# The last head's prompt output row moved into the samples' row of score sums, and the samples' new tokens summed in their output row

## The chip, the cores and the metric

The kernel runs on one core of one Trainium2 chip. The metric is the device time of one execution in microseconds (us). Five engines run side by side, each through its own queue in order: PE (TensorE, matmuls, with weight loads shown apart as PEld), DVE (VectorE), ACT (ScalarE), POOL (GpSimd) and SP (SyncE, which here only issues DMAs). They wait for one another by semaphores.

## The reference, cut to what matters

One layer of a decoder is computed for a prompt of 256 tokens and for 8 samples of 4 new tokens each (32 rows), with the same weights. One projection gives the inputs of a gated short convolution (mixer A), the queries, keys and values of a dilated windowed attention (mixer B), and two gates. Mixer B has 3 groups of 4 heads of 128 features; a head's output is merged over the three groups by their softmax denominators, which is one softmax over the keys of all three groups. A prompt token attends to prompt tokens. A sample's token attends to the sample's cached keys and to its own new tokens:

```python
kg = jnp.concatenate([kv_prev[g][:, :, 0].astype(x.dtype), kg], axis=1)
vg = jnp.concatenate([kv_prev[g][:, :, 1].astype(x.dtype), vg], axis=1)
o, l = _dilated_band_sample(q[:, :, g], kg, vg, slopes[g], dil)
wg = jax.nn.softmax(jnp.stack(lses), axis=0)
yb = jnp.einsum('gnth,gnthd->nthd', wg, jnp.stack(outs)).reshape(n, t, ATT_OUT).astype(x.dtype)
```

The rest of the layer takes `yb` into a product with `w_branch_b`, then come `w_out`, a layer norm, a gated feed-forward part and a second norm. All inputs are float32.

## The kernel before, in words

**The products.** Nearly all of the time goes into products of weights with the 288 token columns (256 of the prompt, 32 of the samples). Each weight block is 128 outputs by up to 2048 inputs. To keep float32 accuracy each operand is split into a high and a low part, and `mms` (L237) makes three matmuls for each 128 by 128 piece: high with high (L243), high with low (L244), low with high (L245). `product` (L225) takes the next prepared block, prepares another with `prepare` (L185), lets one step of the samples' attention be issued (`next(steps)`), issues the matmuls, and then calls `prompt_step` (L216).

**The weights' way.** `prepare` issues the load of a block by SP into one of three `wst` buffers. In two halves of 1024 columns ACT casts the high part and DVE subtracts to get the low part (`split`, L248, shown at L249), into four `whi` and four `wlo` buffers. A cast can be made as soon as PE has used the half four before it. When casts or subtractions come late, PE stands at L243 or L245.

**The order of the work.** A planner orders each engine's instructions before the run, by the order in which the program gives them and by expected times; the order is then fixed. `behind` and `in_a_row` fix the order of two instructions on one engine by hand. Work beside the products is issued in portions: each product's `prompt_step` issues up to `N_MOVES` (7) items from two lists, `soon` first, then `some_time` (`some_moves`, L209), and takes the prompt's attention one stage further.

**The prompt's attention** (`prompt_attention`, L466) runs head by head while the keys and values of the next head are projected. For a head it issues a row of score matmuls (L478), and in the same row on PE the output matmuls of the head before (`output_row`, L430, L439). Softmax follows. Values and weights are then turned for the output: DVE transposes 32 by 32 blocks (`squares`, L448), and the blocks are moved to their places (`moved`, L460): of sixteen blocks four on the diagonal by POOL, twelve by ACT (L458), which go into `soon`. The output row's result is copied from PSUM by ACT (L444), turned by DVE, moved by twelve DVE copies (L456, in `some_time`) and split into `ybh` and `ybl`. The last of the four heads has no successor, so its output row stands alone on PE (L524), and its moves are not portioned out: twice `some_moves(len(soon))` (L514, L519) issues all that is waiting. It runs while the first products of mixer A's convolution stage go on.

**The samples' attention** (`sample_steps`, L575) is a list of steps, one to a product, from the last query products on until its output row at 666 us in the trace. Cached keys are multiplied by the queries on ACT and POOL (L562, L564) and folded by DVE (L570). `key_sums` (L604) sums over the feature quarters on PE (L599) and scores the new keys (L612), both in one row on PE. `scores` makes the softmax, `weights_by_key` turns the weights. `new_values` turns the new tokens' values into `vn`, `new_output` (L652) multiplies them by their weights in a row of its own (L655), ACT copies the result (`o_sb`), `output_by_feature` turns it by sixteen DVE transposes (L410) into `oT`. Then the cached values are treated as the keys were, and `output` (L660) sums their quarters on PE (L599), adds `oT` on DVE (L666) and splits the samples' columns of `ybh` and `ybl`.

**Memory.** `dd_all` holds 4608 columns of 128 partitions: two buffers `kv` of a head's keys and values (columns 0 to 3456, the second, used by the last head, from 1728 on) and `sw[0]` behind them. `sw[1]` is a tile of its own. Both `sw` hold the samples' sums and weights in turn. After a head's projection ACT issues the DMAs that send its keys and values out (L765, L766).

Of the kernel before, what the change touches and what calls it, by code (L numbers as in the profile page):

```python
# [12 lines left out]
AF = mybir.ActivationFunctionType  # L13
ALU = mybir.AluOpType
# [3 lines left out]
P = 128  # L18
# [63 lines left out]
LATER = 3  # L82

N_MOVES = 7

# [13 lines left out]
def layer_kernel(ctx: ExitStack, tc: tile.TileContext, ins, outs):  # L101
# [103 lines left out]


    soon, some_time = [], []

    def some_moves(n):  # L209
        for _ in range(n):  # L210
            for todo in (soon, some_time):
                if todo:
                    todo.pop(0)()
                    break

    def prompt_step():  # L216
        some_moves(N_MOVES)
        if prompt[0]:
            prompt[1] -= 1
            if prompt[1] <= 0:  # L220
                prompt[1] = next(prompt[0], None)
                if prompt[1] is None:
                    prompt[0] = None
# [186 lines left out]
                behind(dve.transpose(out[b : b + 32, :, a : a + 32], src[a : a + 32, :, b : b + 32]), w_split[1])  # L410
            yield

    def to_features(j):

        squares(o_squares, o_two)
        for c in range(NC):
            to = oT.rearrange("p (a h i c) -> p a c h i", a=2, h=2, c=NC // 2)[:, c % 2, c // 2]
            for d in range(0, P, 32):
                move(some_time, (c * 32, d), to[d : d + 32], o_squares[c * 32 : (c + 1) * 32, :, d : d + 32], True)
        some_time.append(lambda: split(h2(ybh[:, j])[:, :, :P], h2(ybl[:, j])[:, :, :P], h2(oT)))  # L420
# [8 lines left out]

    def output_row():  # L430

        j, v, sums = o_next.pop()
        po = sb(ps, [P, SEQ], "acc")
        row = []
        for h in range(2):
            for b in range(2 + h):
                for c in range(NC):
                    at = slice(c * NW, (c + 1) * NW)
                    row.append(pe.matmul(  # L439
                        po[at, h * P : (h + 1) * P], sT[:, 2 * h + b, at], v[:, b if b <= h else 2 + c],  # L440
                        start=b == 0, stop=b == 1 + h,
                    ))
        for h in range(2):
            act.activation(o_two[:, h], po[:, h * P : (h + 1) * P], AF.Copy, scale=sums[h])  # L444
        to_features(j)
        return row

    def squares(out, src):  # L448
# [11 lines left out]
    def moved(out, src):  # L460

        for a in range(0, P, 32):
            for b in range(0, P, 32):
                move(soon, (a, b), out[b : b + 32, :, a : a + 32], src[a : a + 32, :, b : b + 32])

    def prompt_attention(j, q, kT, vT, k_class):  # L466

        s3 = [att((2 + h) * P) for h in range(2)]
        row = [last_mm[0]]

        for h in range(2):
            near = (1 + h) * P
            for g in range(NG):
                for c in range(NC):
                    at = slice(c * NW, (c + 1) * NW)
                    keys, k = (far_keys(h, g), k_class[g - 1][:, c, : (1 + h) * NW]) if g else (
                        slice(0, near), kT[:, 0, :near])
                    row.append(pe.matmul(  # L478
                        s3[h][at, keys], q[:, g, h * P + c * NW : h * P + (c + 1) * NW], k, start=True, stop=True
                    ))  # L480
        if o_next:
            some_moves(len(soon))
            row += output_row()
        in_a_row(row)
        s_flat = s_all.rearrange("p b k -> p (b k)")
        s = [s_flat[:, : 2 * P], s_flat[:, 2 * P :]]
        pool.memset(s[0][:, P:].rearrange("p (g k) -> p g k", g=NG - 1)[:, :, NW:], -BIG)
        for h in range(2):
            near = (1 + h) * P
            for g in range(NG):  # L490
                at = far_keys(h, g) if g else slice(0, near)
                dve.scalar_tensor_tensor(
                    s[h][:, at], m_far[:, h, g - 1, : (1 + h) * NW] if g else m_near[h], -SLOPE[g][j] / SCALE,
                    s3[h][:, at],
                    ALU.mult, ALU.add,
                )
        sums = []
        for h in range(2):
            st = sb(wk, [P, 4], "st", bufs=4)
            dve.reduce_max(st[:, 0:1], s[h], AX.X)  # L500
            dve.tensor_scalar_mul(st[:, 1:2], st[:, 0:1], -SCALE)
            act.activation(s[h], s[h], AF.Exp, bias=st[:, 1:2], scale=SCALE, accum_out=st[:, 2:3])
            dve.reciprocal(st[:, 3:4], st[:, 2:3])
            sums.append(st[:, 3:4])
        v = v_two[j % 2]
        squares(v_squares[:, :2], vT[:, 0, :SEQ].rearrange("p (b k) -> p b k", b=2))
        for g in range(1, NG):
            squares(
                v_squares[:, 2:, (g - 1) * NI : g * NI].rearrange("p c (h i) -> p c h i", i=32),
                vT[:, g, :SEQ].rearrange("p (h i c) -> p c h i", h=2, c=NC),  # L510
            )
        moved(v, v_squares)
        if j == NH - 1:
            some_moves(len(soon))  # L514
        yield 1
        squares(s_squares, s_all)
        moved(sT, s_squares)
        if j == NH - 1:
            some_moves(len(soon))  # L519
        yield 2  # L520

        o_next.append((j, v, sums))
        if j == NH - 1:
            in_a_row([last_mm[0]] + output_row())  # L524


    dd_all = sb(big, [P, KD * T], "dd")
    kv = dd_all[:, : 2 * 2 * NG * T].rearrange("p (b c g t) -> p b c g t", b=2, c=2, g=NG)
    sw = [dd_all[:, 2 * 2 * NG * T :], sb(wk, [P, (NB + 1) * NH * NS], "sw", bufs=1)]

    n_half = NH * NT * P // 2
    halves = [dd_all[:, h * n_half : (h + 1) * n_half] for h in range(2)]
# [42 lines left out]
    def sample_steps():  # L575
# [3 lines left out]
        s_key = sw[0][:, : (NG + 1) * P].rearrange("p (g r) -> p g r", r=P)  # L579
        sT, sTn = s_key[:, :NG], s_key[: NG * NS, NG]  # L580

        vn = dd_all[: NG * NS, 2 * n_half : 2 * n_half + NH * P].rearrange("p (j d) -> p j d", j=NH)
        o_sb = sw[0][:, NG * P + P + NH * P : NG * P + 2 * P + NH * P]
        oT = sw[1][:, NB * P :]

        n = NH * NQ * NS
        sums_k, sums_v = (
# [16 lines left out]
        def key_sums():  # L604
            pk = att(NG * P)
            row = []
            for g in range(NG):
                row += four_parts(pk[:, g * P : (g + 1) * P], sums_k[g], start=True, stop=True)

            ps_s.append(att(NG * NS))  # L610
            row += [
                pe.matmul(  # L612
                    ps_s[0][j * NS : (j + 1) * NS, k * NS : (k + 1) * NS], q_s[:, k, j, :],
                    k_s[:, k, j, :], start=True, stop=True,
                )
                for k in range(NG) for j in range(NH)
            ]
            in_a_row([last_mm[0]] + row)
            act.copy(by_key, pk)
# [26 lines left out]
        def new_values():  # L646
            yield from turned(vn, v_s.rearrange("p j g r -> p j (g r)"), NG * NS)

        def output_by_feature():
            yield from turned(oT.unsqueeze(1), o_sb.unsqueeze(1))  # L650

        def new_output():  # L652
            p = att(P)
            in_a_row([last_mm[0]] + [
                pe.matmul(p[j * NS : (j + 1) * NS], sTn[:, j * NS : (j + 1) * NS], vn[:, j, :], start=True, stop=True)  # L655
                for j in range(NH)
            ])
            act.copy(o_sb, p)

        def output():  # L660
            po = att(P)
            row = [last_mm[0]]
            for g in range(NG):
                row += four_parts(po, sums_v[g], start=g == 0, stop=g == NG - 1)
            in_a_row(row)
            dve.tensor_tensor(oT, oT, po, ALU.add)  # L666
            split(*(h3(t)[:, :, :, P:] for t in (ybh, ybl)), oT.rearrange("p (j a h) -> p j h a", j=NH, h=2))

        for i, o in enumerate(range(0, P, 32)):
            if i == 1:  # L670
# [36 lines left out]
        for which, order in (("ck", far + near), ("cv", near + far)):  # L707
            for i, (n, t) in enumerate(order):
                for h in range(2):
                    when = now + (2 * i + h) * PACE[0] // PACE[1]  # L710
                    if t == h == 0:
                        at(when - LATER, load, which, n)
                    at(when, multiply, u, h, which, n, t)
                    at(when + 1, fold, u, h)
                u += 1
            if which == "ck":
                for d, what in ((2, key_sums), (4, scores), (9, new_output)):
                    at(when + d, what)
                for d, blocks in (
                    ((-6, -5, -4), new_values), ((3, 3, 4, 4), scores_by_row), ((6, 6, 7, 7), weights_by_key),  # L720
                    ((10, 11, 12, 13), output_by_feature),
                ):
                    what = by_fours(blocks)
                    for n in d:
                        at(when + n, what)
                now = when + 9
# [597 lines left out]
```

## Time and profile before

Three runs took 1708.12 to 1709.82 us, with a median of 1709.02.

| What | us |
|---|---|
| profiled execution, its own time | 1709.05 |
| its span in the trace | 1707.3 |
| PE busy | 1699.9 |
| DVE busy | 1192.2 |
| ACT busy | 941.3 |
| POOL busy | 387.6 |

The granted TensorE clock is 0.999 of full speed. A matmul of 288 columns shows 0.29 us from start to modelled end, but the next starts 0.12 us after it: matmuls overlap in the pipeline, so the cost of a matmul is read from the distance of starts, and not from its duration. In a row of the timeline stand the start and the length of a stretch of like instructions, the engine and line, the operation, the tiles (output, arrow, inputs), the shapes and the count, and in square brackets the engine's idle time before it with what ended it. In the prompt's part (about 100 to 250 us) ACT is busy 18 to 19 us of 20 in several stretches; DVE has 19.86 of 20 at 260 to 280 us.

### The profile page before, as it was taken

The numbers are of one execution on the slowest core, as the hardware profiler recorded it, in microseconds if no ns is written. First come the engines' busy times: TensorE is split into PE (matmuls) and PEld (weight loads), VectorE is DVE, ScalarE is ACT, GpSimd is POOL, SyncE is SP. The second block draws the span as 40 slices with busy tenths as digits, with TensorE's granted clock in tenths as the row PEclk, the third lists the DMA queues.
The fourth block names the chain that finished last, engine by engine and source line by source line (L and its number), as shares of the span: only waits on it lengthen the run. The fifth ranks groups of instructions, "written<-read, shape, count | busy, mean of one in ns | idle before, by whom it ended". The sixth has DMA issues, their size and how long they took to land.

```text
span 1707.3 us, 34334 instructions
## 1 busy us (share of the span) xinstructions
PE 1699.9 (100%) x14148; PEld 1694.4 (99%) x14148; DVE 1192.2 (70%) x1575; ACT 941.3 (55%) x1665; POOL 387.6 (23%) x510
## 2 busy tenths in 40 slices
PE   9999999999999999999999999999999999999998
PEld 9999999999999999999999999999999999999998
DVE  5477889978887675455788887855686554555575
ACT  5578876645666564444546555543555443344454
POOL 1123333202222210001453332300111100011164
PEclk9999999999999999999999999999999999999999
DMA  8788877676778886677766666666666566666663
GB/s 297 287 298 316 335 304 265 235 280 249 272 292 335 326 310 249 222 261 253 274 236 226 228 247 230 229 233 222 228 231 257 222 229 238 249 223 231 223 242 135
DMA packets 59068, 436.16 MB, mean 255 GB/s; under 512 B 7648, under 2 KB 11232, under 8 KB 19168
## 3 DMA queue, kind: packets, MB, share of 16 engines
q1 hardware_dynamic: 57472, 429.85, 67.6%
q10 hardware_dynamic: 1440, 4.13, 0.7%
q8 instruction: 110, 1.80, 0.4%
q14 instruction: 46, 0.38, 0.1%
HBM read 427.50 MB, written 94.53 MB: 306 GB/s over the span
## 4 chain that ended last, share of the span: by engine, by line
PE 98%; ACT 1%; DVE 1%; DMA 0%; issue 0%; SPq 0%; DVEq 0%
PE acc L243 32%; PE acc L245 32%; PE acc L244 32%; PE acc L331 1%; DMA wst<-in_w_in 0%; ACT yal L458 0%; DVE wlo L249 0%; PE acc L439 0%; PE att L478 0%; ACT yah L458 0%; ACT whi L249 0%; DVE dd L570 0%; PE long L978 0%; DVE yah L990 0%; PE acc L985 0%
## 5 line engine op out<-in xcount | busy, mean ns | idle before, releaser
L249 DVE TENSOR_TENSOR wlo<-wst,whi 128x1024 fp32r<-128x1024 f32 (+1 forms) x578 | 738.1, 1280 | 405.2 <-ACT whi L249 402.1
L249 ACT CAST whi<-wst 128x1024 fp32r<-128x1024 f32 (+1 forms) x578 | 588.6, 1021 | 679.9 <-PE acc L244 611.0
L243 PE MATMUL acc<-xh,whi 128*128 128x288 f32 (+1 forms) x3216 | 921.1, 286 | 0.0
L245 PE MATMUL acc<-xh,wlo 128*128 128x288 f32 (+1 forms) x3216 | 920.5, 286 | 0.4 <-DVE wlo L249 0.4
L244 PE MATMUL acc<-xl,whi 128*128 128x288 f32 (+1 forms) x3216 | 920.3, 286 | 0.0
L243 PEld LDWEIGHTS acc<-xh,whi 128*128 128x128 f32 x3216 | 607.8, 189 | 1.3 <-issue 1.2
L245 PEld LDWEIGHTS acc<-xh,wlo 128*128 128x128 f32 x3216 | 607.8, 189 | 0.8 <-DVE wlo L249 0.8
L244 PEld LDWEIGHTS acc<-xl,whi 128*128 128x128 f32 x3216 | 607.8, 189 | 0.0
L245 PE MATMUL acc<-yah,wlo 128*128 128x288 f32 x1216 | 347.7, 286 | 0.0
L244 PE MATMUL acc<-yal,whi 128*128 128x288 f32 x1216 | 347.7, 286 | 0.0
L243 PE MATMUL acc<-yah,whi 128*128 128x288 f32 x1216 | 347.6, 286 | 0.0
L245 PEld LDWEIGHTS acc<-yah,wlo 128*128 128x128 f32 x1216 | 229.8, 189 | 0.0
L244 PEld LDWEIGHTS acc<-yal,whi 128*128 128x128 f32 x1216 | 229.8, 189 | 0.0
L243 PEld LDWEIGHTS acc<-yah,whi 128*128 128x128 f32 x1216 | 229.8, 189 | 0.0
L794 POOL COPY qk_s<-u 128x2 f32<-128x2 f32 x44 | 36.8, 836 | 535.5 <-ACT u L1083 412.7
L782 DVE SCALAR_TENSOR_TENSOR cy<-u,prm,cy 128x304 f32<-128x304 f32 x120 | 72.6, 605 | 5.6 <-ACT cy L780 2.4
L564 POOL TENSOR_TENSOR cache<-cache,dd 128x1024 f32<-128x1024 f32 x16 | 34.1, 2134 | 93.4 <-DMA cache<-in_cv 55.8
L249 ACT CAST yah<-ya 128x288 fp32r<-128x288 f32 x76 | 32.6, 429 | 27.5 <-DVE ya L805 11.1
L564 POOL TENSOR_TENSOR cache<-cache,qk_s 128x1024 f32<-128x1024 f32 x16 | 32.7, 2045 | 53.7 <-DMA cache<-in_ck 40.6
L853 POOL TENSOR_TENSOR ya<-ya,dd 128x288 f32<-128x288 f32 x16 | 13.7, 858 | 133.8 <-DVE ya L852 132.8
L775 POOL COPY u<-prm 128x16 f32<-128x16 f32 x60 | 42.2, 704 | 4.6 <-DMA prm<-in_prm 4.6
L562 ACT ACTIVATE cache<-cache,qk_s 128x128 f32<-128x128 f32 x128 | 40.8, 392 | 0.0
(224 smaller groups left out, 1190.8 us busy)
## 6 DMA issues: line engine op xcount, KB each, us to landing
wst<-in_w_in SPq DMA_DIRECT2D x112, 1024.0 KB, 5.0
wst<-in_w_up SPq DMA_DIRECT2D x88, 1024.0 KB, 4.9
wst<-in_w_down SPq DMA_DIRECT2D x32, 1024.0 KB, 4.9
cache<-in_ck SPq DMA_DIRECT2D x18, 1024.0 KB, 7.8
cache<-in_cv SPq DMA_DIRECT2D x18, 1024.0 KB, 8.5
wst<-in_w_a SPq DMA_DIRECT2D x16, 1024.0 KB, 4.9
wst<-in_w_out SPq DMA_DIRECT2D x16, 1024.0 KB, 4.9
wst<-in_w_down SPq DMA_DIRECT2D x16, 768.0 KB, 4.4
```

The source lines that it names most:

```text
L243: pe.matmul(out, hi[:, c, :], xh_k, start=k == 0, stop=False)
L244: pe.matmul(out, hi[:, c, :], xl_k, start=False, stop=False)
L245: last_mm[0] = pe.matmul(out, lo[:, c, :], xh_k, start=False, stop=k == nk - 1)
L249: return act.copy(hi, src), dve.tensor_tensor(lo, src, f32(hi), ALU.subtract)
L331: i = pe.matmul(o[b], first_w(term == 2, b, k), xk, start=k == 0 and term == 0, stop=k == KD - 1 and term == 2,)
L562: behind(act.activation(o[:, a, b], t[:, a, b], AF.Copy, scale=w[:, a, b : b + 1]), w_split[0])
L564: behind(pool.tensor_tensor(o, t, w.unsqueeze(3).broadcast_to([P, *n]), ALU.mult), w_split[1])
L775: pool.tensor_copy(tail[:, :, 0:2], prm[:, state : state + 2 * NB].rearrange("p (b r) -> p b r", b=NB))
L782: dve.scalar_tensor_tensor(y, u[:, i : i + YW], prm[:, w0 + i : w0 + i + 1], y, ALU.mult, ALU.add)
L794: pool.tensor_copy(dst[:, 0:2], u[:, SEQ : SEQ + 2])
L853: pool.tensor_tensor(m, m, ma[:, i], ALU.add)
```

## The change

Three things are done together.

- The last head's output row no longer stands alone. Its moves go through the lists as those of the other heads. `key_sums` first issues whatever is left in the lists, then puts the output row ahead of its own row on PE. For that the last head's turned weights and values get a place that lives on: `late_p` and `late_v` in `dd_all`, columns 2048 to 3456; and the output's intermediate tiles one in `sw[0]` and `sw[1]` (`late_homes`). From then on `prompt_step` issues three items a product (`N_LATE`). A new step, `prompt_features`, issues what is left of them six steps later.
- `new_output` and `output_by_feature` go, with `o_sb` and `oT`. In `output`, after the quarters of the first group, sixteen matmuls add the new tokens' part directly, by feature, into the same PSUM tile (four heads by four blocks of 32 features). The addition on DVE goes; the split reads PSUM.
- `vn` moves from `dd_all` to the place of the samples' queries and keys (`qk_s`), and is made later: at steps 10 to 12 after the last key fold in place of 6 to 4 ahead of it.

```diff
 N_MOVES = 7
+N_LATE = 3
...
     def prompt_step():
-        some_moves(N_MOVES)
+        some_moves(N_LATE if all_heads[0] else N_MOVES)
...
-        j, v, sums = o_next.pop()
+        j, v, p, sums = o_next.pop()
+        homes = late_homes if j == NH - 1 else (o_two, o_squares, oT)
...
-                        po[at, h * P : (h + 1) * P], sT[:, 2 * h + b, at], v[:, b if b <= h else 2 + c],
+                        po[at, h * P : (h + 1) * P], p[:, 2 * h + b, at], v[:, b if b <= h else 2 + c],
...
-        v = v_two[j % 2]
+        v, p = (late_v, late_p) if j == NH - 1 else (v_two[j % 2], sT)
...
         moved(v, v_squares)
-        if j == NH - 1:
-            some_moves(len(soon))
         yield 1
         squares(s_squares, s_all)
-        moved(sT, s_squares)
-        if j == NH - 1:
-            some_moves(len(soon))
+        moved(p, s_squares)
         yield 2
 
-        o_next.append((j, v, sums))
-        if j == NH - 1:
-            in_a_row([last_mm[0]] + output_row())
+        o_next.append((j, v, p, sums))
...
+    late_p, late_v = (
+        dd_all[:, a * P : b * P].rearrange("p (b k) -> p b k", k=P) for a, b in ((16, 16 + MB), (16 + MB, 27))
+    )
+    late_homes = tuple(
+        sw[i][:, a : a + SEQ].rearrange("p (b d) -> p b d", b=2) if k < 2 else sw[i][:, a : a + SEQ]
+        for k, (i, a) in enumerate(((0, 4 * P), (0, 6 * P), (1, 7 * P)))
+    )
...
-        vn = dd_all[: NG * NS, 2 * n_half : 2 * n_half + NH * P].rearrange("p (j d) -> p j d", j=NH)
-        o_sb = sw[0][:, NG * P + P + NH * P : NG * P + 2 * P + NH * P]
-        oT = sw[1][:, NB * P :]
+        vn = qk_s[: NG * NS, : NH * P].rearrange("p (j d) -> p j d", j=NH)
...
+            some_moves(len(soon + some_time))
+            all_heads[0] = True
+            row = output_row() + row
             ps_s.append(att(NG * NS))
...
-        def new_output():
-            p = att(P)
-            in_a_row([last_mm[0]] + [
-                pe.matmul(p[j * NS : (j + 1) * NS], sTn[:, j * NS : (j + 1) * NS], vn[:, j, :], start=True, stop=True)
-                for j in range(NH)
-            ])
-            act.copy(o_sb, p)
+        def prompt_features():
+            some_moves(len(some_time))
...
                 row += four_parts(po, sums_v[g], start=g == 0, stop=g == NG - 1)
+                if g == 0:
+                    for j in range(NH):
+                        at = slice(j * NS, (j + 1) * NS)
+                        row += [
+                            pe.matmul(
+                                po[b : b + 32, at], vn[:, j, b : b + 32], sTn[:, at], start=False, stop=False,
+                            )
+                            for b in range(0, P, 32)
+                        ]
             in_a_row(row)
-            dve.tensor_tensor(oT, oT, po, ALU.add)
-            split(*(h3(t)[:, :, :, P:] for t in (ybh, ybl)), oT.rearrange("p (j a h) -> p j h a", j=NH, h=2))
+            split(*(h3(t)[:, :, :, P:] for t in (ybh, ybl)), po.rearrange("p (j a h) -> p j h a", j=NH, h=2))
...
-                for d, what in ((2, key_sums), (4, scores), (9, new_output)):
+                for d, what in ((2, key_sums), (4, scores), (8, prompt_features)):
...
-                    ((-6, -5, -4), new_values), ((3, 3, 4, 4), scores_by_row), ((6, 6, 7, 7), weights_by_key),
-                    ((10, 11, 12, 13), output_by_feature),
+                    ((10, 11, 12), new_values), ((3, 3, 4, 4), scores_by_row), ((6, 6, 7, 7), weights_by_key),
```

More of the change, by code (lines that the diff above doesn't have):

```diff
@@ L207, in layer_kernel @@
     soon, some_time = [], []
+    all_heads = [False]
     def some_moves(n):
@@ L411, in turned, with to_features @@
             yield
-    def to_features(j):
+    def to_features(j, o_two, o_squares, oT):
         squares(o_squares, o_two)
@@ L443, in output_row @@
         for h in range(2):
-            act.activation(o_two[:, h], po[:, h * P : (h + 1) * P], AF.Copy, scale=sums[h])
-        to_features(j)
+            act.activation(homes[0][:, h], po[:, h * P : (h + 1) * P], AF.Copy, scale=sums[h])
+        to_features(j, *homes)
         return row
@@ L647, in new_values @@
             yield from turned(vn, v_s.rearrange("p j g r -> p j (g r)"), NG * NS)
-        def output_by_feature():
-            yield from turned(oT.unsqueeze(1), o_sb.unsqueeze(1))
-        def new_output():
-            p = att(P)
-            in_a_row([last_mm[0]] + [
-                pe.matmul(p[j * NS : (j + 1) * NS], sTn[:, j * NS : (j + 1) * NS], vn[:, j, :], start=True, stop=True)
-                for j in range(NH)
-            ])
-            act.copy(o_sb, p)
+        def prompt_features():
+            some_moves(len(some_time))
         def output():
```

## The prediction

> **What bounds the kernel now.** I read the page's engine table first, then the list of waits, then the timeline of PE.
>
> ```profile
> span 1707.3 us, 34334 instructions
> PE 1699.9 (100%) x14148; PEld 1694.4 (99%) x14148; DVE 1192.2 (70%) x1575; ACT 941.3 (55%) x1665; POOL 387.6 (23%) x510
> PEclk9999999999999999999999999999999999999999
> PE 98%; ACT 1%; DVE 1%; DMA 0%; issue 0%; SPq 0%; DVEq 0%
> ```
>
> PE is busy for the whole span at full granted clock, and the chain that ended last is 98% PE. So a change counts only as far as it alters what PE issues, or how long PE stands still. PE's own waits over the whole run are these (what waited, for what; us in total, times, longest):
>
> ```profile
> PE acc L261 <- DVE cy L258: 1.2, 1, 1.2
> PE acc L331 <- ACT whi L298: 0.5, 1, 0.5
> PE acc L245 <- DVE wlo L249: 0.4, 1, 0.4
> PE acc L985 <- DVE yah L990: 0.2, 1, 0.2
> PE acc L983 <- DVE yah L990: 0.2, 1, 0.2
> ```
>
> Four of them are at the start and the tail, which the change does not touch. One, for the lower half of a split weight (L249), lies in the stage that the change rewrites. The timeline of PE shows what the waits and the odd rows really cost, in start-to-start distances:
>
> ```profile
> 394.09 0.29 PE L243 MATMUL acc<-xh,whi 128*128 128x288 f32 x1
> ...
> 394.70 0.29 PE L245 MATMUL acc<-xh,wlo 128*128 128x288 f32 x1
> 394.92 0.42 PE L655 MATMUL att<-dd 96*32 96x128 f32 x8
> ...
> 395.50 0.29 PE L244 MATMUL acc<-xl,whi 128*128 128x288 f32 x1
> ...
> 241.52 0.29 PE L244 MATMUL acc<-xl,whi 128*128 128x288 f32 x1
> 242.20 0.39 PE L245 MATMUL acc<-xh,wlo 128*128 128x288 f32 x1 [0.39 <-DVE wlo L249]
> 242.43 0.29 PE L243 MATMUL acc<-xh,whi 128*128 128x288 f32 x1
> ...
> 244.88 0.29 PE L245 MATMUL acc<-xh,wlo 128*128 128x288 f32 x1
> ...
> 246.55 0.29 PE L244 MATMUL acc<-xl,whi 128*128 128x288 f32 x1
> 246.78 0.39 PE L245 MATMUL acc<-xh,wlo 128*128 128x288 f32 x1
> 247.00 0.29 PE L243 MATMUL acc<-xh,whi 128*128 128x288 f32 x1
> ```
>
> From 394.09 to 394.70 are five steps in 0.61 us: the pace is 0.122 us per matmul, and two undisturbed steps are 0.244. Whatever stands above that is loss.
>
> **The change, part by part.**
>
> The row of the samples' new tokens (L655) goes. From 394.70 to 395.50 its row takes 0.80 us where two steps would be 0.244, so it costs 0.56 us of PE. Its copy out of PSUM, 16 transposes and the addition at L666 go with it; they are ACT and DVE work and gain nothing by themselves.
>
> The output row of the last head goes from 245 us into the row of the samples' score sums at 352 us. Standing alone it costs 1.67 - 0.244 = 1.43 us (244.88 to 246.55). What the same 40 instructions cost inside another row is seen in the chain, where head 0's output row follows the next head's scores:
>
> ```profile
> 149.02 1.14 PE att L478 x48
> 150.16 1.09 PE acc L439 x40
> ...
> 352.65 0.79 PE att L599 x24
> 353.44 0.19 PE att L612 x24
> ```
>
> There they take 1.09 us. So going into and out of a row of narrow matmuls costs 1.43 - 1.09 = 0.34 us, and the change saves it once here. (In the 0.56 of L655 it is already contained.)
>
> The sixteen matmuls that are added to the samples' output row at 666 us are 32 instructions, since the trace shows two for each (x8 for the four of L655). Their form is 96 rows by 32 columns against 32 moving columns. The nearest row is L612, 128 by 32 against 32: 24 in 0.19 us, 8 ns each, so 32 cost 0.25 us. The other bound is L655 itself, 128 moving columns: 0.56 - 0.34 = 0.22 us for 8, 27 ns each, 0.87 us for 32. I take 0.25, because L612 has the same moving size and the same four column positions; below zero it cannot go, since the instructions are new.
>
> A rule of the Trainium skill speaks against this value: "TensorE: Matmul & The Clock Gate", section "Wait — 56ns, not 53.3ns?", says that starts of matmuls never come closer than about 25 ns however few columns move. By it the 32 would take an estimated 0.80 us and the whole gain below would shrink by 0.55 us. The trace's 8 ns for L612 disagrees with it for tiles of 32 columns.
>
> Now the stall. It comes from a burst on ACT: for the last head all queued moves are issued at once (the two `some_moves(len(soon))`), twelve of them just ahead of a weight cast:
>
> ```profile
> 234.75 1.05 ACT L249 CAST whi<-wst 128x1024 fp32r<-128x1024 f32 x1
> 235.82 4.00 ACT L458 COPY yah<-yah 32x160 f32<-32x160 f32 x12
> 239.85 1.04 ACT L249 CAST whi<-wst 128x1024 fp32r<-128x1024 f32 x1
> ...
> 240.92 1.23 DVE L249 TENSOR_TENSOR wlo<-wst,whi 128x1024 fp32r<-128x1024 f32 x1 [3.87 <-ACT whi L249]
> ```
>
> The cast waits 4.00 us behind the moves, DVE idles 3.87 us for it, and PE needs the difference before DVE has it. From 241.52 to 242.43 that is 0.91 - 0.244 = 0.67 us. After the output row comes a second one, 246.55 to 247.00: 0.45 - 0.244 = 0.21 us. With the change the 24 moves go seven to a product, as for the heads before, which show no PE wait in the list; so the burst is spread, and of DVE's work in the tight stretch the last head's squares, its twelve copies (L456) and one split leave. I count both stalls as gone: 0.88 us. Bounds: all of it stays (0), or it becomes longer (the second rival).
>
> Where the moved work lands:
>
> ```profile
> 220.00:240.00 20.00, 20.00 (x234) 19.48 (x233) 15.77 (x33) 18.43 (x53) 11.11 (x16) 1.00 0.86 341
> 240.00:260.00 20.00, 19.61 (x186) 18.89 (x185) 18.82 (x32) 14.08 (x31) 4.39 (x9) 1.00 0.70 263
> 260.00:280.00 20.00, 20.00 (x166) 20.00 (x165) 19.86 (x28) 13.97 (x29) 7.46 (x7) 1.00 0.81 306
> 340.00:360.00 20.00, 20.00 (x204) 19.81 (x203) 12.97 (x17) 10.30 (x19) 1.36 (x4) 1.00 0.68 257
> 360.00:380.00 20.00, 20.00 (x165) 20.00 (x164) 17.12 (x37) 9.16 (x13) 1.36 (x4) 1.00 0.68 263
> ...
> 254.81 0.43 DVE L450 STREAM_TRANSPOSE yal<-yah 128x256 f32<-128x256 f32 x1
> 255.68 1.55 DVE L456 COPY yal<-yal 32x64 f32<-32x64 f32 x7
> 260.80 1.00 DVE L456 COPY yal<-yal 32x64 f32<-32x64 f32 x5
> 262.97 0.42 DVE L249 TENSOR_TENSOR ybl<-yal,ybh 128x256 fp32r<-128x256 f32 x1
> ```
>
> (Columns of a window: its length, then busy us of PE, PEld, DVE, ACT and POOL.) The squares, twelve copies and the split's DVE half are 0.43 + 1.55 + 1.00 + 0.42 = 3.4 us. They leave the stretch where DVE is full (18.82 and 19.86 of 20) for 352 to 385 us, where DVE has 7.0 + 2.9 = 9.9 us free in 40. At three to a product (`N_LATE`) that is 0.6 us in each product. I cost it at nothing: the cover is DVE's idle time. The twelve transposes of the new values go from 310 us to where the sixteen of the old row were, about 400 us, so DVE there has less to do than before. The waits that this adds are short ones: the copies out of the output row now wait for the score sums behind it on PE (0.98 us), since the new home of the row (`late_homes`) is where one of the sums lay. No DMA is added or moved on SP's, ACT's or POOL's queues.
>
> Sum: 0.56 + 0.34 + 0.88 - 0.25 = 1.53 us. The profiled execution took 1709.05 us (span 1707.3 and 1.75 around it), the median of the runs 1709.02, so both give 1707.5 us.
>
> **A new wait that speaks against it.** `late_p` and `late_v` lie in `dd_all` from column 2048 to 3456, and the last head's keys and values are columns 1728 to 3456 of the same tile. So the first move into `late_v` cannot run before the values have been sent out:
>
> ```profile
> 228.98 0.34 ACTq L766 DMA_DIRECT2D out_o_v<-dd  x1
> 231.83 1.07 ACT L458 COPY yal<-yal 32x192 f32<-32x192 f32 x3
> DMA to landing us min/median/max: 5.7/6.6/6.7
> ```
>
> Before, moves of values that need the last transposes ran from 231.83. After, they must wait for 228.98 + 6.6 = 235.6 us, and everything behind them on ACT, weight casts among it, may wait up to 3.8 us. The diagonal copies on POOL, and behind them the products that DVE folds, wait likewise.
>
> The Trainium skill, "DMA: Bandwidth & Descriptors", section "Anatomy of one DMA — SWDGE (gpsimd) path", fits a DMA with about 2.0 us plus its bytes at 436 GB/s, an estimated 3.0 us for these 432 KB. By it the values would be out at 232.0 us and this rival would cost nothing; that fit is for another issue path, and the trace's 5.7 to 6.7 us is twice it.
>
> **Rivals.**
>
> 1. The stalls stay although the moves are spread, because ACT was near full before (18.4 of 20 us from 220 to 240, more than DVE) and of the 24 moves that it made by 239.85 some fourteen (two products' worth) would still be ahead of that cast. Then 1.53 - 0.88 = 0.65 us are gained: 1708.4 us. The dearer price for the new matmuls alone (0.87) gives 1708.1. Both are within my case's neighbourhood.
>
> 2. Slower: the wait for the values' DMA. If ACT's order has the seven moves ahead of the cast that was at 234.75, then ACT stands to 235.6, moves to 235.6 + 7 x 0.35 = 238.1, casts to 239.1, and DVE has the lower half at 240.4. PE reaches that half at 241.64 (the unstalled time of 242.20) less 24 x 0.122 = 238.7 us. So PE would stand 1.7 us in place of 0.88 and the sum is 0.65 - 1.7: slower by 1.05 us, 1710.1. With a second batch of seven ahead of it as well, PE would stand 4.2 us: 1712.6. The rival decides from a stall of 0.65 us on (the change then gains nothing); 0.2%, or 3.4 us, needs one of 4.1 us. For it speaks that the moves come first in the program. Against it: nothing holds that cast back, since its buffer is free when PE has used the half four before it, at 238.7 - 3 x 24 x 0.122 = 229.9 us, and an order made out by expected times would then place it ahead of moves that are not ready.
>
> 3. Faster by 0.2%: PE has only the losses named here (about 2 us in all between 20 and 1690 us), so no mechanism gives it; only a shift between executions could.
>
> 4. That the change does not do what it says: if the row at 352 waited for late moves, PE would stand there. But 24 moves at seven a product are through by about 260 us. I give it nothing of its own.
>
> **How the numbers follow.** My case, with rival 1 as its upper edge, has 0.72: 1707.5, its own range 1706.9 to 1708.5. Rival 2 with a short stall (1708.5 to 1710.4) has 0.14, with a long one (over 0.2% slower, the schedule otherwise disturbed included) 0.11. Faster by 0.2% has 0.03. A difference of 0.2% (3.4 us) is about the least that a measurement of this kernel tells from none; the runs shown spread over 1.7 us. Hence faster 0.03, same 0.86, slower 0.11. The range for 8 in 10 is 1706.6 to 1710.2: the lower end is the sum plus half the runs' spread, the upper takes in the one-batch stall.
>
> **What would show it.** In the changed kernel: no row L655 near 395 us, and L243 to L244 there at pace; L439 for the last head directly ahead of L599 at about 352 us with one entry and one exit; 32 narrow instructions in the row at 666 us adding about 0.25 us (0.8 would bear out the 25 ns floor); no PE wait for `wlo` between 235 and 285 us. Wrong, if the list of waits has ACT on `out_o_v` for some us near 232 and PE on `wlo` by more than 0.65 us, or if a PE wait appears between 352 and 400 us.

## The result, and the profile after

The changed kernel takes 1714.03 us (median of 7 runs, 1712.74 to 1714.98) against 1709.02 us before: a ratio of 1.0029, with a 95% interval of 1.002 to 1.0039. It is 5.0 us slower. I had forecast 1.5 us faster, and 1714.03 lies above my range. The profiled execution took 1713.75 us, its span is 1712.0 us. (Line numbers move: L243 to L245 are now L245 to L247, L249 is L251, L439 is L442, L458 is L461, L599 is L602.)

The page of the changed kernel, its head and the shares of the chain that ended last:

```profile
span 1712.0 us, 34365 instructions
PE 1701.5 (99%) x14172; PEld 1696.8 (99%) x14172; DVE 1189.9 (70%) x1558; ACT 941.5 (55%) x1664; POOL 383.8 (22%) x510
PE 98%; DMA 1%; DVE 0%; ACT 0%; issue 0%; DVEq 0%; ACTq 0%
```

A DMA stands in the chain with 1%, where there was 0% before: it is `out_o_v`, the one that sends out a head's values. The list of waits, of PE and then of ACT between 220 and 260 us (what waited, for what; us in total, times, longest):

```profile
PE acc L247 <- DVE wlo L251: 2.1, 1, 2.1
PE acc L245 <- ACT whi L251: 1.9, 1, 1.9
...
ACT dd L461 <- DMA out_o_v<-dd: 4.6, 1, 4.6
```

The timeline of ACT in that stretch shows what is queued behind this wait:

```profile
226.71 0.34 ACTq L771 DMA_DIRECT2D out_o_v<-dd  x1
...
231.13 0.51 ACT L505 ACTIVATE yal<-yal,st 128x256 f32<-128x256 f32 x1 [2.18 <-DVE st L504]
...
236.30 0.71 ACT L461 COPY dd<-yal 32x192 f32<-32x192 f32 x2 [4.57 <-DMA out_o_v<-dd]
237.03 0.61 ACT L505 ACTIVATE yal<-yal,st 128x384 f32<-128x384 f32 x1
...
237.77 1.79 ACT L461 COPY dd<-yal 32x192 f32<-32x192 f32 x5
239.58 1.99 ACT L251 CAST whi<-wst 128x1024 fp32r<-128x1024 f32 x2
```

From 231.7 to 236.3 us ACT stands before the first move into `late_v`. Behind that move wait six more moves, the second exponential (L505) among them, and two weight casts. Now PE, by the starts of its matmuls:

```profile
238.44 0.29 PE L247 MATMUL acc<-xh,wlo 128*128 128x288 f32 x1
240.68 0.39 PE L245 MATMUL acc<-xh,whi 128*128 128x288 f32 x1 [1.95 <-ACT whi L251]
240.91 0.29 PE L246 MATMUL acc<-xl,whi 128*128 128x288 f32 x1
243.28 0.61 PE L247 MATMUL acc<-xh,wlo 128*128 128x288 f32 x1 [2.09 <-DVE wlo L251]
243.68 0.45 PE L245 MATMUL acc<-xh,whi 128*128 128x288 f32 x1
...
246.32 0.29 PE L247 MATMUL acc<-xh,wlo 128*128 128x288 f32 x1
```

From 238.44 to 243.28 are three steps in 4.84 us where 0.37 would do: 4.47 us are lost in two stalls. From 243.28 to 246.32 are twelve steps in 3.04 us where 1.47 would do, 0.24 us a step: another 1.57 us. In that second part PE waits for nothing. The windows of the changed kernel show why (length, busy us of PE, PEld, DVE, ACT and POOL, then the granted clock):

```profile
238.00:240.00 2.00, 0.73 (x6) 0.51 (x5) 0.68 (x1) 1.93 (x6) 1.08 (x4) 1.00 0.03 12
...
242.00:244.00 2.00, 0.72 (x3) 0.72 (x4) 2.00 (x2) 1.94 (x6) 0.14 (x1) 0.72 0.00 0
244.00:246.00 2.00, 2.00 (x10) 2.00 (x10) 2.00 (x3) 1.96 (x4) 0.00 (x0) 0.50 0.22 41
246.00:248.00 2.00, 2.00 (x17) 2.00 (x16) 2.00 (x3) 2.00 (x7) 0.00 (x0) 0.92 0.90 381
```

The granted clock falls to one half at 242.9 us, within the second stall, and comes back 3.4 us later, at 246.3 us. In the page's row of 40 slices, each 43 us long, none of this shows.

What was saved by the rows came as the sum had it, but for one term. Timeline of PE in the changed kernel, at the row of score sums and at the samples' output row:

```profile
356.20 0.29 PE L247 MATMUL acc<-xh,wlo 128*128 128x288 f32 x1
...
358.72 0.29 PE L246 MATMUL acc<-xl,whi 128*128 128x288 f32 x1
...
670.11 0.29 PE L247 MATMUL acc<-yah,wlo 128*128 128x288 f32 x1
...
670.57 0.45 PE L667 MATMUL att<-dd,qk_s 96*32 96x32 f32 x30
...
671.65 0.29 PE L246 MATMUL acc<-xl,whi 128*128 128x288 f32 x1
```

The same two places in the kernel before:

```profile
352.37 0.29 PE L245 MATMUL acc<-xh,wlo 128*128 128x288 f32 x1
...
353.79 0.29 PE L244 MATMUL acc<-xl,whi 128*128 128x288 f32 x1
...
665.74 0.29 PE L245 MATMUL acc<-yah,wlo 128*128 128x288 f32 x1
...
666.97 0.29 PE L244 MATMUL acc<-xl,whi 128*128 128x288 f32 x1
```

The merged row costs 2.52 - 0.24 = 2.28 us; apart, the two rows cost 1.43 and 1.42 - 0.24 = 1.18, so 0.33 us are saved (forecast 0.34). The samples' output row grew from 1.23 to 1.54 us: 0.31 us for 32 instructions, 9.7 ns each (forecast 0.25). The row of the new tokens is gone (0.56), the old stalls at 242 and 247 us are gone (0.88). So -0.33 - 0.56 - 0.88 + 0.31 + 4.47 + 1.57 = +4.58 us; the spans differ by 4.7 and the medians by 5.0.

### The profile page after: what moved, and what is told of

It reads as the page before. It is cut to its first block, busy times and chain, and to the rows that moved or that the text cites. A ratio compares the mean times of both kernels' runs of the same rounds, so it can differ in the third digit from the quotient of the medians.

```text
span 1712.0 us, 34365 instructions
## 1 busy us (share of the span) xinstructions
PE 1701.5 (99%) x14172; PEld 1696.8 (99%) x14172; DVE 1189.9 (70%) x1558; ACT 941.5 (55%) x1664; POOL 383.8 (22%) x510
## 4 chain that ended last, share of the span: by engine, by line
PE 98%; DMA 1%; DVE 0%; ACT 0%; issue 0%; DVEq 0%; ACTq 0%
PE acc L245 32%; PE acc L247 32%; PE acc L246 32%; PE acc L333 1%; DMA out_o_v<-dd 1%; PE acc L263 0%; DVE wlo L251 0%; PE acc L442 0%; PE att L481 0%; PE long L983 0%; ACT dd L461 0%; DVE yah L995 0%; ACT whi L251 0%; PE acc L990 0%; PE att L602 0%; PE att L908 0%
## 5 line engine op out<-in xcount | busy, mean ns | idle before, releaser
L251 DVE TENSOR_TENSOR wlo<-wst,whi 128x1024 fp32r<-128x1024 f32 (+1 forms) x578 | 740.6, 1284 | 409.1 <-ACT whi L251 405.8
L251 ACT CAST whi<-wst 128x1024 fp32r<-128x1024 f32 (+1 forms) x578 | 588.7, 1021 | 682.4 <-PE acc L246 609.5
L245 PE MATMUL acc<-xh,whi 128*128 128x288 f32 (+1 forms) x3216 | 921.7, 287 | 1.9 <-ACT whi L251 1.9
L247 PE MATMUL acc<-xh,wlo 128*128 128x288 f32 (+1 forms) x3216 | 921.1, 286 | 2.1 <-DVE wlo L251 2.1
L245 PEld LDWEIGHTS acc<-xh,whi 128*128 128x128 f32 x3216 | 608.4, 189 | 3.1 <-ACT whi L251 2.4
L247 PEld LDWEIGHTS acc<-xh,wlo 128*128 128x128 f32 x3216 | 608.5, 189 | 2.3 <-DVE wlo L251 2.3
L247 PE MATMUL acc<-yah,wlo 128*128 128x288 f32 x1216 | 347.7, 286 | 0.0
L245 PE MATMUL acc<-yah,whi 128*128 128x288 f32 x1216 | 347.6, 286 | 0.0
L247 PEld LDWEIGHTS acc<-yah,wlo 128*128 128x128 f32 x1216 | 229.8, 189 | 0.0
L245 PEld LDWEIGHTS acc<-yah,whi 128*128 128x128 f32 x1216 | 229.8, 189 | 0.0
L569 POOL TENSOR_TENSOR cache<-cache,dd 128x1024 f32<-128x1024 f32 x16 | 34.4, 2150 | 92.7 <-DMA cache<-in_cv 77.2
L251 ACT CAST yah<-ya 128x288 fp32r<-128x288 f32 x76 | 32.6, 429 | 23.6 <-POOL ya L858 9.0
L569 POOL TENSOR_TENSOR cache<-cache,qk_s 128x1024 f32<-128x1024 f32 x16 | 32.6, 2043 | 54.6 <-DMA cache<-in_ck 54.1
```

The source lines that it names most:

```text
L245: pe.matmul(out, hi[:, c, :], xh_k, start=k == 0, stop=False)
L247: last_mm[0] = pe.matmul(out, lo[:, c, :], xh_k, start=False, stop=k == nk - 1)
L251: return act.copy(hi, src), dve.tensor_tensor(lo, src, f32(hi), ALU.subtract)
L569: behind(pool.tensor_tensor(o, t, w.unsqueeze(3).broadcast_to([P, *n]), ALU.mult), w_split[1])
```

## The experiments

Theory A: the first move into `late_v` waits for the landing of the last head's values, ACT's order has two weight casts behind the moves, PE stands for these, and its clock falls. Rival B: the loss comes from the moves being spread among the casts, with or without the DMA. Rival C: it comes from the new tokens' part.

To compare the runs by one number I take from each trace the distance between the starts of the same two L245 matmuls (L247 after the change), number 501 and number 901 of that line; in the kernel before they stand at 214.23 and 367.14 us. Everything of the last head lies between them, and nothing of the new tokens' two rows at about 395 and 666 us.

| kernel | 501st to 901st, us | median of its runs, us | before, beside it |
|---|---|---|---|
| before | 152.91 | 1709.02 | |
| changed | 157.73 | 1714.03 | 1709.02 |
| tokens_only | 152.96 | 1708.94 | 1709.03 |
| late_only | 158.98 | 1714.61 | 1709.03 |
| no_ov | 151.70 | 1708.09 | 1709.03 |
| v_last | 151.70 | 1707.87, again 1707.32 | 1709.03, 1708.65 |
| ov_twice | 157.84 | 1713.77 | 1708.65 |
| copy_later | 154.19 | 1708.72 | 1708.65 |
| few_moves (3) | 153.24 | 1709.82 | 1708.65 |
| five_moves (5) | 154.70 | 1711.95 | 1709.16 |

**Which part of the change: tokens_only and late_only.** In tokens_only the last head is as before (both `some_moves(len(soon))` and its own row on PE are back). In late_only the new tokens keep their own row:

```diff
-                    ((10, 11, 12), new_values), ((3, 3, 4, 4), scores_by_row), ((6, 6, 7, 7), weights_by_key),
+                    ((5, 6, 7), new_values), ((3, 3, 4, 4), scores_by_row), ((6, 6, 7, 7), weights_by_key),
+                    ((10, 11, 12, 13), output_by_feature),
```

> Only the second part of the change: the new tokens in the samples' output row, the last head's row as before. Theory A: -0.56 + 0.30 = -0.26 us, the old stall at 242 us stays, so 1708.8 us, not to be told from before. Rival C (the loss comes from the new tokens' part, its later transposes or the place of vn): 1712 us or more.

> Only the first part: the last head's row with the score sums, the new tokens in a row of their own as before (their values turned at steps 5 to 7, since their old place is taken). Theory A: the whole loss is here, with ACT's wait for the values' DMA: 1714.0 + 0.26 = 1714.3 us. Rival C: 1708 to 1709 us.

Measured: 1708.94 us (ratio 0.9998, 0.9989 to 1.0007) and 1714.61 us (1.0024, 1.0015 to 1.0033). Rival C falls: the new tokens' part alone is not to be told from before, and its trace still has the old wait. The last head's part alone has the whole loss, with ACT's wait of 4.3 us for the DMA. The waits of tokens_only (first row) and of late_only:

```profile
PE acc L247 <- DVE wlo L251: 0.4, 1, 0.4
```

```profile
PE acc L247 <- DVE wlo L251: 2.1, 1, 2.1
PE acc L245 <- ACT whi L251: 1.6, 1, 1.6
...
ACT dd L461 <- DMA out_o_v<-dd: 4.3, 1, 4.3
```

**Without the DMA: no_ov.**

```diff
-        act.dma_start(outs["o_v"][j].rearrange("p (g t) -> p g t", g=NG), vT)
+        if j < NH - 1:
+            act.dma_start(outs["o_v"][j].rearrange("p (g t) -> p g t", g=NG), vT)
```

> The changed kernel without the DMA that sends out the last head's values (that part of the output is left out). Theory A (ACT stands for the landing of this DMA, weight casts stand behind it, PE stands for them and then runs at half clock): ACT's wait of 4.6 us near 232 us is gone, PE has no wait on weights between 235 and 285 us, and the gains are left: 0.34 (row merged) + 0.56 (row gone) - 0.30 (32 added instructions as the changed kernel's trace shows them) + 0.88 (old stalls) = 1.5 us, so about 1707.5 us against 1709.0 before. Rival B (spreading the 24 moves puts them ahead of the casts, with or without the DMA): still a PE wait of about 2 us and more, 1711 to 1714 us.

Measured: 1708.09 us (0.9994, 0.9986 to 1.0003), 0.6 us above the expectation. PE has no wait on weights in the list, and the stretch takes 151.70 us, 1.21 less than before: the 0.33 of the row and the 0.88 of the old stalls. Rival B falls: moves in the same number and in nearly the same order, with nothing to wait for, cost nothing. ACT in no_ov:

```profile
230.78 0.71 ACT L461 COPY dd<-yal 32x192 f32<-32x192 f32 x2 [2.08 <-DVE st L504]
231.52 0.51 ACT L505 ACTIVATE yal<-yal,st 128x256 f32<-128x256 f32 x1
...
232.15 1.79 ACT L461 COPY dd<-yal 32x192 f32<-32x192 f32 x5
233.96 0.61 ACT L505 ACTIVATE yal<-yal,st 128x384 f32<-128x384 f32 x1
...
234.58 1.98 ACT L251 CAST whi<-wst 128x1024 fp32r<-128x1024 f32 x2
```

This row of work also answers why the casts lay behind the moves. Seven moves and then two casts is the order here, where nothing holds the moves up, and in the changed kernel the order differs only in where the two exponentials stand among the moves. So the order was made as if the values were out almost as soon as the moves were due. (That is inferred from the two orders; the planner's times themselves are not in the trace.)

**The moves later: v_last.** All DMAs are there; the last head's value moves go into the list behind its weight moves, a product later.

```diff
-        moved(v, v_squares)
+        if j < NH - 1:
+            moved(v, v_squares)
         yield 1
         squares(s_squares, s_all)
         moved(p, s_squares)
+        if j == NH - 1:
+            moved(v, v_squares)
         yield 2
```

> The changed kernel with all its DMAs, but the last head's twelve value moves put into the list behind its twelve weight moves, one product later, when the values have landed outside. Theory A: the wait is gone because it is over before the first move is due: about 1707.5 us, 1.5 us faster than before and 6.5 faster than the changed kernel. Rival B (number and spreading of the moves, not the DMA): 1711 to 1714 us, with a PE wait somewhere between 240 and 265 us.

> The version with the value moves behind the weight moves, once more, to narrow the interval against the kernel before: theory A gives 1707.5 us, a ratio of 0.9991; the first time it was 1707.87. No PE wait on weights between 20 and 1690 us.

Measured: 1707.87 us (0.9992, 0.9983 to 1.0000), and the second time 1707.32 us (0.9994, 0.9985 to 1.0003). The medians lie 1.16 and 1.33 us below those of before beside them, near the 1.5 forecast for the change itself; but the intervals reach 1.0000 and 1.0003, so the times alone do not show a gain over the kernel before. Against the changed kernel's 1714.03 it is over 6 us faster. ACT in v_last, where the casts now run in the time that was lost:

```profile
231.04 1.03 ACT L251 CAST whi<-wst 128x1024 fp32r<-128x1024 f32 x1
...
233.60 1.03 ACT L251 CAST whi<-wst 128x1024 fp32r<-128x1024 f32 x1
...
235.32 2.33 ACT L461 COPY dd<-yah 32x160 f32<-32x160 f32 x7 [0.39 <-issue]
```

Its DMA lands as late as ever (9.5 us after its issue at 226.1, 235.6 us), POOL waits 3.8 us for it, and PE shows no wait from 20 to 1690 us.

**The landing moved: copy_later and ov_twice.** In copy_later two copies from memory to memory go out with later weight loads, among them the one that was under way together with `out_o_v`; in ov_twice the DMA is issued twice.

```diff
-        if n >= 20 and n % 10 in (0, 3, 7):
+        if n >= 20 and (n % 10 in (0, 3, 7) and n not in (33, 37) or n in (45, 48)):
```

```diff
         act.dma_start(outs["o_v"][j].rearrange("p (g t) -> p g t", g=NG), vT)
+        if j == NH - 1:
+            act.dma_start(outs["o_v"][j].rearrange("p (g t) -> p g t", g=NG), vT)
```

> The changed kernel with two of the copies from memory to memory moved to other weight loads, among them the one issued at 222.96 us (1 MB, 10.3 us to landing), which is under way together with the values' DMA. If the DMA lands late (9.6 us) because of this company, it lands after 5 to 7 us, at 232 to 234 us, ACT waits 0 to 2 us, and PE's stall is gone or under 1 us: 1707.5 to 1709.5 us. If the landing does not depend on it: 1714 us.

> The changed kernel with the DMA of the last head's values issued twice, so that the first value move waits for both. Theory A: the landing moves from 236.3 us to some 2 to 4 us later, ACT's wait of 4.6 us and PE's first stall of 2.1 us grow by the same amount, one for one: 1716 to 1718 us, with the half clock behind it as in the changed kernel. Rival B (the moves' number, not the landing): 1714 us as without.

copy_later took 1708.72 us (1.0001, 0.9992 to 1.0010): 5 us of loss are gone though no engine has more or less to do. ACT in copy_later:

```profile
226.08 0.34 ACTq L771 DMA_DIRECT2D out_o_v<-dd  x1
...
233.17 0.71 ACT L461 COPY dd<-yal 32x192 f32<-32x192 f32 x2 [4.85 <-DMA out_o_v<-dd]
```

The values land after 7.1 us and not 9.6, ACT goes on 3.1 us sooner, and PE loses 0.9 us at 239 and 1.6 us at 252 us, 2.5 in all, at full clock: 154.19 against the 151.70 of a stretch without stalls. I had expected less than 1 us, and a wait of ACT of at most 2; ACT idles as long as before, only at another time.

ov_twice missed its purpose. Its time is 1713.77 us (1.0029, 1.0017 to 1.0040), which the expectation gave to rival B, but not for B's reason: the second issue itself waited for the first landing, on ACT's queue.

```profile
236.00 0.34 ACTq L773 DMA_DIRECT2D out_o_v<-dd  x1
236.39 0.62 ACT L505 ACTIVATE yal<-yal,st 128x384 f32<-128x384 f32 x1 [5.09 <-DMA out_o_v<-dd]
...
237.00 1.98 ACT L251 CAST whi<-wst 128x1024 fp32r<-128x1024 f32 x2
```

The value moves went behind the casts this time, which fits an order made from expected landings, but ACT stood for 5.09 us all the same, and PE's stalls came in smaller pieces up to 254 us. It does not price a later landing. It shows the clock again: with stalls of 1.1 and 1.4 us between 251.6 and 254.5 us, it is full up to 255.72 us and then one half:

```profile
252.30:255.72 3.42, 1.69 (x11) 1.48 (x12) 2.90 (x3) 3.35 (x6) 1.11 (x1) 1.00 0.06 24
255.72:259.13 3.41, 3.41 (x17) 3.41 (x16) 3.33 (x7) 3.41 (x11) 0.00 (x0) 0.50 0.62 235
```

**How many moves stand between the landing and the casts: few_moves and five_moves.**

```diff
-        some_moves(N_LATE if all_heads[0] else N_MOVES)
+        some_moves(N_LATE if all_heads[0] or last_head[0] else N_MOVES)
```

(`last_head` is set once the last head's value moves are in the list; five_moves has 5 there.)

> The changed kernel with three moves a product in place of seven for the last head. ACT still waits for the landing at about 236 us, but four moves fewer stand between it and the casts: 1.4 us sooner. Theory A: PE's first stall shrinks from 2.1 to about 0.7 us, the second stays at 1 to 2.3. If the half clock comes from PE's idle time in a short stretch, it is shorter or absent: 1709.5 to 1712 us. If the half clock belongs to any stall of 2 us it stays at about 1.4 us: 1712 to 1713.

> The changed kernel with five moves a product for the last head, between the seven of the changed kernel and the three that gave two short PE waits (1.4 us of loss together, granted clock full). Theory A: two moves fewer than in the changed kernel stand between the landing at about 236 us and the casts, 0.7 us: PE's first wait is about 1.4 us, the second 1 to 2.3, together 2.4 to 3.7 us. Idle of that size within 4 us is where the half clock should begin (it came after 2.7 us of idle in the run with the DMA issued twice, and not after 1.6): 1710 to 1713 us. Rival B (number of moves as such): no order between three, five and seven.

Measured: 1709.82 us (1.0010, 1.0000 to 1.0019) and 1711.95 us (1.0017, 1.0007 to 1.0027). ACT's wait is the same in both (4.3 and 4.6 us). The stretch is 1.5, 3.0 and 6.0 us longer than 151.70 with three, five and seven moves, so the order that theory A expects holds. PE's waits in few_moves, then in five_moves (the lines of the changed kernel are one further on here):

```profile
PE acc L248 <- DVE wlo L252: 0.8, 1, 0.8
PE acc L246 <- ACT whi L252: 0.2, 1, 0.2
```

```profile
PE acc L246 <- ACT whi L252: 1.3, 1, 1.3
...
PE acc L248 <- DVE wlo L252: 0.8, 1, 0.8
```

In both, the granted clock is 1.00 throughout the stretch; in five_moves I had expected the half clock to begin, and it did not. The step from five to seven moves is 0.7 us of ACT's work and 3.0 us of time: the first stall grows by 0.7 us, the second by 1.3, and the clock takes 1.57, less a third small stall of 0.35 us that only five_moves has. The median of five_moves lies 1.1 us above that of v_last plus its 3.0 us (1.6 with v_last's second runs); part of that may be the tail, from the last L248 to the end, which took 16.7 us in its profiled execution and 15.4 in that of v_last.

## Why the prediction was wrong

**What held.** The row that goes (0.56) is gone from its place in the changed kernel's trace. The entry and exit saved (0.33 for 0.34) and the old stalls (0.88) show together in no_ov and v_last, with 1.21 us less in the stretch and no wait left. Nothing of the late row is seen on PE after 352 us: DVE's idle time there covers it, as the sum assumed. The floor of about 25 ns between starts that the Trainium skill gives ("TensorE: Matmul & The Clock Gate", section "Wait — 56ns, not 53.3ns?") does not hold for these narrow tiles: 32 instructions took 0.31 us.

**The step that failed** is the choice between my forecast and rival 2. I named the DMA wait, its place and its price, and then argued it down: "nothing holds that cast back, since its buffer is free", so "an order made out by expected times would then place it ahead of moves that are not ready". The buffer was free, but seven moves, the waiting one first, stood ahead of two casts all the same. The order fits expected landings that are nearer than the real ones, which is inferred, as said at no_ov. So the sum put at nothing a wait that cost PE 4.47 us in stalls and 1.57 at half clock, 6.04 in all, against the 1.46 that the rest gained. The trace of before had the landing (5.7 to 6.7 us), but no trace shows what a planner expects; that part of the argument had no row under it. With rival 2 at 0.14 and 0.11 the chances were set on that argument.

**The terms of rival 2 that were mis-sized.** For one batch of seven moves it gave a stall of 1.7 us; PE lost 6.04.

- The landing: 235.6 forecast, 236.3 measured. In the changed kernel ACT issued the DMA 2.3 us sooner (226.71 for 228.98) since fewer moves were ahead of it, but it took 9.6 us. copy_later shows that the copy beside it has part in this.
- ACT behind the landing: forecast seven moves, with the cast at 238.1. The second exponential, 0.73 us with its read, stood among them, and the casts began at 239.58.
- The subtraction on DVE: forecast 1.23 us. In the changed kernel the first of two took 2.5 us, while POOL multiplied:

```profile
240.66 3.70 DVE L251 TENSOR_TENSOR wlo<-wst,whi 128x1024 fp32r<-128x1024 f32 x2 [1.98 <-ACT whi L251]
```

```profile
240.25 1.89 POOL L569 TENSOR_TENSOR cache<-cache,qk_s 128x1024 f32<-128x1024 f32 x1
```

(3.70 us for two, of which the second took 1.2; the first is DVE's, the second fence POOL's timeline.) POOL too had stood behind the landing, for 3.9 us, before it came to this product. The trace shows that the subtraction had to wait for POOL's product to end: of the lower halves of 1024 columns, 40 start while POOL makes such a product of a cache tile (L569), and every one of them ends 1.08 to 1.19 us after that product, however much of it was left; they take up to 2.94 us. Alone a subtraction takes 1.23. So the landing came into the second stall by POOL too.
- The clock, 1.57 us, was in no rival at all.

So the place and the chain were those of rival 2, at a price that it did not hold. The stalls alone, 4.47 us against a net gain of 1.46 from the rest, would have made +3.0 us, above my range already but within 0.2%; the clock carried the change over that.

## What to carry to other kernels

When scratch is put into memory that a DMA is still reading, the first write waits for the landing, and everything queued behind that write on its engine waits too; look at what stands behind it, and price the wait by the landing in the trace, not by where a sensible order would put the work. An order that is fixed before the run holds only as far as its expected times do: v_last costs PE nothing, because its value moves come a product later, behind the landing. In a kernel bound by PE, two stalls close together can cost more than their sum (the last section has when), so the price of a new wait must include the clock.

## What the runs showed of the hardware

The granted TensorE clock fell to one half after 4.4 us of idle in 4.8 us (changed kernel), 4.1 in 4.5 (late_only), and after 2.4 us of idle between 251.6 and 254.5 us in ov_twice; it stayed at full in five_moves after 2.4 us of idle between 238.0 and 240.9 us. The half clock lasted 3.4 us in the changed kernel, 3.4 in ov_twice and 6.8 in late_only (242.31 to 249.14 us), at 0.24 us a matmul for 0.12. The Trainium skill, "TensorE: Matmul & The Clock Gate", section "What's actually happening", has the clock set by windows of about 3.4 us that run freely, so that it depends on where the idle time falls in them. The traces agree: in every run's trace, each change of the granted clock lies a whole number of steps of 3.41 us behind its first rise to full speed. Cut the trace into windows at these steps. Then most of the idle time of the changed kernel (first fence) falls into one window, and so does most of that of ov_twice (the two rows shown at that run); the idle time of five_moves (second fence) is spread over two:

```profile
239.49:242.90 3.41, 0.51 (x2) 0.30 (x2) 2.24 (x1) 3.32 (x7) 2.52 (x3) 1.00 0.00 0
242.90:246.31 3.41, 3.03 (x12) 3.03 (x13) 3.41 (x4) 3.34 (x7) 0.00 (x0) 0.50 0.17 41
```

```profile
236.63:240.05 3.42, 2.13 (x16) 1.70 (x14) 1.44 (x3) 3.35 (x7) 2.23 (x8) 1.00 0.12 48
240.05:243.46 3.41, 2.58 (x21) 2.58 (x22) 3.41 (x2) 3.31 (x8) 2.53 (x1) 1.00 0.00 0
```

In all eleven traced executions, every window at full clock in which PE was busy for 1.73 us or less was followed by half clock (0.51 in the changed kernel, 1.69 in ov_twice), and none with 2.13 us or more was. The half clock ended behind a window with 3.03 us busy (changed kernel), and went on for a second one behind 2.77 (late_only). That section of the Trainium skill names an idle window as the condition; here a window with half its time in work was still followed by half clock. Where the windows lie is seen only in the trace, so before a run a price for the half clock can only be given as a range. The runs of late_only spread from 1708.34 to 1715.40 us; whether that comes from the windows is open, since one execution of it was traced.
